# Zero matmuls and a new load order at the start of a hybrid decoder step, and attention scores in two full-height passes

## The chip, the core and the metric

The kernel runs on one core of one Trainium2 chip. The metric is device time in microseconds of one execution, lower is better. Engines are called as the profile calls them: PE is TensorE (matmul), PEld its weight loads, DVE VectorE, ACT ScalarE, POOL GpSimd, SP the engine whose queue issues the DMAs. The trace also gives the clock that TensorE was granted, as a share of 2.4 GHz; its two levels are 1.2 and 2.4 GHz.

## The reference

One layer of a decoder for 1024 prompt tokens and 64 sample tokens (8 requests of 8), model width 1024, float32:

- RMSNorm, then one combined projection into q, k, v of a sliding-window attention (8 heads of 64, 2 key heads) and into the parts of an mLSTM (4 heads);
- sliding-window attention with sinks, where each block of 128 queries reads its own and the previous block of keys:

```python
s = jnp.einsum('bnqhgd,bnkhd->bnhgqk', q, k) * (HEAD_DIM ** -0.5)
s = jnp.where(mask, s, -jnp.inf)
m = jnp.maximum(jnp.max(s, axis=-1, keepdims=True), sink)
p = jnp.exp(s - m)
p = p / (jnp.sum(p, axis=-1, keepdims=True) + jnp.exp(sink - m))
```

- the mLSTM in chunks with a carried state, head norm and output gate; both joined by one output projection and a residual add;
- cross-attention to 256 memory tokens (4 heads of 64), a SwiGLU feed-forward of 2816, a last RMSNorm. The sample tokens do the same with cached keys, values and states.

## The kernel before

Activations lie feature-major (128 features on the partitions, 1088 tokens along the row), cut in columns into `CH` = 384, 384 and 320. Every large product is made of three float32r products: both operands are split exactly into a high and a low part (`split`, L100 to L109: high part by ScalarE, L102 or L108, or by VectorE with a scale, L106; low part by VectorE or GpSimd, L103 or L109), and `mm3` adds high x high, high x low and low x high in PSUM. `mm` (L85) records every matmul, so in the trace products are told apart by their tiles.

Weights come through `load_w` (L111): one DMA into `wraw` (two buffers), then a split into `whi` and `wlo` (two buffers each). `tok_w` does so for the token-major weights `win_a` and `win_b`.

The start (L157 to L203): for each of eight feature tiles the x tile is loaded (L162) and split, even tiles with ScalarE and odd ones with VectorE for the high part. Behind tile 0 the first two weight tiles `win_f[0]` and `win_f[1]` are loaded whole. ScalarE squares the x tiles (L174), GpSimd adds the first half of the squares and VectorE the second (L178). The two first column tiles, in six PSUM accumulators, run along with the arrival of x (144 matmuls). Then a float32 product with ones sums the squares over the features, ScalarE makes rstd of it, and the token-major part begins with `wa = tok_w(win_a, ...)`, whose raw parts use the two `wraw` buffers, and `tok_gemm`.

The mLSTM and the four q tiles follow. In the sliding-window stretch `swa_unit` (L684) does one block of 128 queries and one pair of q tiles, 16 units in the order block, pair. A generator (`wout_mlstm`) gives matmul work that is set between the units, `nfill[u]` pieces behind unit u. The scores of a unit:

```python
for j2 in range(2):
    cs = slice(j2 * 256, j2 * 256 + 256)
    for z, (a, b_) in enumerate(((qh, khi), (qh, klo), (ql, khi))):
        for kv in range(2):
            pr = slice(kv * 64, kv * 64 + 64)
            mm(sc[kv][:, cs], a[pr, j2, :], b_[pr, k0:k0 + 256], z == 0, z == 2)
```

These are twelve matmuls of 64 rows: head 0 of the pair on partitions 0 to 63, head 1 on 64 to 127. VectorE then adds the mask and takes the maxima (L703), ScalarE the exponentials (L622), VectorE scales (L627), TensorE transposes (`pt`, L717), ScalarE copies (`pp`, L718), and the product with the values follows (`o`). `cross_unit` (8 units, each two blocks and one pair of heads) has the same form with `kvhl` in place of the keys: maxima L866, exponentials L887, scales L891, transposes L897. `swa_sample` and `cross_sample` do the sample tokens in float32.

Buffers: slots of one size under a tag; tag `c` has nine, which hold x tiles, keys (`khi`, `klo`), values (`vp`), the mLSTM values, `kvf`, `pp` and later feed-forward operands. `tmp` has ten. PSUM: `mm` three banks, `pt` two, `sc` two, `o` one.

Order: the tile framework orders the instructions of each engine by the order of the program and by when its own model has their operands ready, allocates slots as they come free, and sets all semaphores. Engines then run their queues in that order.

Of the kernel before, what the change touches and what calls it, by code (L numbers as in the profile page):

```python
# [9 lines left out]
F32 = mybir.dt.float32  # L10
# [5 lines left out]
P = 128  # L16
D = 1024
NK = D // P                 # feature tiles of the model width
TP = 1024                   # prompt tokens
TS = 64                     # sample tokens (8 requests x 8)  # L20
T = TP + TS
NB = TP // P                # prompt token blocks
CH = [(0, 384), (384, 768), (768, 1088)]
CHE = [(0, 416), (416, 832), (832, 1088)]   # where the last one ends the kernel
FT = 22                     # feature tiles of the FFN
GROUPS = [(0, 2), (2, 6), (6, 10), (10, 14), (14, 18), (18, 22)]
EPS = 1e-6
NEG = -1.0e30

# columns of the vectors packed by the host  # L30
# [3 lines left out]
# columns of the constants  # L34
C_ID, C_ONE, C_CAUS, C_CAUSS, C_BM, C_M0, C_M1 = 0, 128, 256, 384, 448, 456, 712
C_N = 968
# columns of the constants for the gates
# [5 lines left out]
def tile_hymba_step(  # L43
# [51 lines left out]

    def gcol(base, k):
        return vv[:, base + k:base + k + 1]

# [1 line left out]
    def split(hi, lo, src, scale=None, eng=None):  # L100
        if scale is None:
            A.activation(hi, src, AF.Copy)  # L102
            (eng or V).tensor_tensor(lo, src, hi.bitcast(F32), ALU.subtract)  # L103
        else:
            if eng is V:
                V.tensor_scalar_mul(hi, src, scale)  # L106
            else:
                A.activation(hi, src, AF.Copy, scale=scale)  # L108
            V.scalar_tensor_tensor(lo, src, scale, hi.bitcast(F32), ALU.mult, ALU.subtract)  # L109

# [12 lines left out]
    def load_ahead(srcs):  # L123
        """The weights in the order of their use, each loaded one step ahead of it."""
        todo, ahead = iter(srcs), []

        def step():
            for src, eng in todo:
                ahead.append(load_w(src, 8, eng=eng))
                break  # L130

        def next_w():
            step()
            return ahead.pop(0)

        step()
        return next_w
# [19 lines left out]
    # ================= stage 1: x, split; sums of squares =================  # L157
    nc.scalar.preload_act_table_set("natural_log_exp_and_others")
    xs, xr = [], []
    for k in range(NK):  # L160
        xr.append(slot("cm"[k % 2], [T], name="xraw"))
        nc.sync.dma_start(xr[k], xT[k])  # L162
        hi, lo = slot("x", [T], F32R, name="xhi"), slot("x", [T], F32R, name="xlo")
        split(hi, lo, xr[k], gcol(V_MIX, k), V if k % 2 else A)
        xs.append((hi, lo))
        if k == 0:
            w = load_w(win_f[0], NK)
        if k == 0:
            w1 = load_w(win_f[1], NK)
    nc.sync.dma_start(c, cst)  # L170
    sums = []
    for k in range(NK):
        sq = slot("q", [T], name="sq")
        A.activation(sq, xr[k], AF.Square)  # L174
        if k % 4 == 0:
            sums.append(sq)
        else:
            (G if k < 4 else V).tensor_tensor(sums[-1], sums[-1], sq, ALU.add)  # L178
    rstd = slot("r", [T], name="rstd")
    # the first two tiles run along with the arrival of x  # L180
# [24 lines left out]
    # token-major rstd  # L205
# [19 lines left out]

    def tok_w(src, n, per, tags):
        parts = []
        for k0 in range(0, NK, per):
            tag = tags[k0 // per]
            raw = wp.tile([P, per, n], F32, tag="wraw", name="wrawt", bufs=2)  # L230
            nc.sync.dma_start(raw, src[:, k0:k0 + per, :])
            hi, lo = slot(tag[0], [per, n], F32R, name="wthi"), slot(tag[-1], [per, n], F32R, name="wtlo")
            split(hi, lo, raw)
            parts.append((hi, lo))
        return lambda k: (parts[k // per][0][:, k % per, :], parts[k // per][1][:, k % per, :])
# [11 lines left out]
    wa = tok_w(win_a, 264, 4, "qm")  # L247
# [108 lines left out]
    # rows (block, head) of prompt; rows (head) of sample  # L356
# [40 lines left out]
    # the weight of the state before the block, as rows  # L397
# [33 lines left out]
    # the upper half of the partitions holds the odd heads  # L431
# [20 lines left out]
    # M4: mq pair 0, mq pair 1, mk pair 0, mk pair 1; later the head outputs  # L452
# [4 lines left out]
    # the heads' norm weights with the half of sigmoid(x) = (1 + tanh(x / 2)) / 2  # L457
# [42 lines left out]
    def mlstm_S(blk, m, c0, bc, caus):  # L500
        """S^T[s, t] of the four heads, weighted."""
        dd = bc
        G.tensor_tensor(dd[:m], caus.unsqueeze(1).to_broadcast([m, 4, m]), bc[:m], ALU.subtract)
        for h in range(4):
            A.activation(dd[:m, h, :], dd[:m, h, :], AF.Exp, bias=gg[:m, blk * 4 + h:blk * 4 + h + 1])
        kq = [scps(), scps()]
        for h in range(4):
            pr = slice((h % 2) * 64, (h % 2) * 64 + 64)
            mm(kq[h % 2][:m, (h // 2) * m:(h // 2) * m + m], M4[2 + h // 2][pr, c0:c0 + m], M4[h // 2][pr, c0:c0 + m])
        S = tmp([4, m], name="S")  # L510
        for h2 in range(2):
            V.tensor_tensor(S[:m, h2::2], kq[h2][:m, 0:2 * m].rearrange("p (j t) -> p j t", j=2),
                            dd[:m, h2::2], ALU.mult)
        return S
# [102 lines left out]
    def softmax_pieces(pieces, mx, nbias, es=None):  # L617
        """P = exp(0.125 s + bias) / (sum + es) in place for the (row, piece) scores."""
# [65 lines left out]
    def swa_unit(blk, jp):  # L684
        k0 = max(0, (blk - 1) * P)
        mask = c[:, C_M0:C_M0 + 256] if blk == 0 else c[:, C_M1:C_M1 + 256]
        qhl = tmp([2, 2, P], F32R, name="qhl")
        qh, ql = qhl[:, 0], qhl[:, 1]
        for j2 in range(2):
            split(qh[:, j2, :], ql[:, j2, :], qc[2 * jp + j2][:, blk * P:blk * P + P])  # L690
        sc = [scps(), scps()]
        for j2 in range(2):
            cs = slice(j2 * 256, j2 * 256 + 256)
            for z, (a, b_) in enumerate(((qh, khi), (qh, klo), (ql, khi))):
                for kv in range(2):
                    pr = slice(kv * 64, kv * 64 + 64)
                    mm(sc[kv][:, cs], a[pr, j2, :], b_[pr, k0:k0 + 256], z == 0, z == 2)
# [50 lines left out]
    class Next:  # L748
        """Operands of the GEMM behind a norm: (y * g) split; rstd goes on its output."""
# [68 lines left out]
    for u in range(2 * NB):  # L818
        if u == 0:
            swa_sample()  # L820
        swa_unit(u // 2, u % 2)
# [6 lines left out]
    kvhl = slot("c", [4, 256], F32R, name="kvhl")  # L828
    kvh, kvl = kvhl[:, 0:2], kvhl[:, 2:4]
    split(kvh, kvl, kvf[:, 0:2])  # L830
# [5 lines left out]
    # weights of this stage in the order of their use  # L836
# [31 lines left out]
    def cross_unit(pair, f):  # L868
        """Two blocks of prompt tokens, one pair of heads."""
        bs = slice(pair * 256, pair * 256 + 256)  # L870
        qhl = tmp([2, 256], F32R, name="qhl")
        split(qhl[:, 0], qhl[:, 1], xq[f][:, bs])
        sc = [scps(), scps()]
        for i in range(2):
            ts = slice(i * P, i * P + P)
            for z, (a, b_) in enumerate(((0, kvh), (0, kvl), (1, kvh))):
                for h2 in range(2):
                    pr = slice(h2 * 64, h2 * 64 + 64)
                    mm(sc[h2][:, i * 256:i * 256 + 256], qhl[pr, a, ts], b_[pr, f, :], z == 0, z == 2)
# [168 lines left out]
def _consts():  # L1048
# [19 lines left out]
    # sample window: rows (request of the pair, kv, group, token)  # L1068
# [13 lines left out]
def _tiles(w, cols=None):  # L1082
    """[K, F] -> [F/128, 128, K/128, 128]"""
# [5 lines left out]
def _pack(i):  # L1089
# [23 lines left out]
    for base, g in ((V_MIX, a["g_mix"][0]), (V_CROSS, a["g_cross"][0]), (V_FFN, a["g_ffn"][0]),  # L1113
# [5 lines left out]
    s = a["attn_sinks"][0].reshape(2, 2, 2)          # kv, pair, j2  # L1119
# [56 lines left out]
```

## Time and profile before

| | us |
|---|---|
| median of 3 runs | 1387.66 |
| lowest and highest run | 1380.97 and 1389.8 |
| span of the profiled execution, first to last instruction | 1380.3 |
| TensorE busy in it | 1343.5 (97%) |
| VectorE, ScalarE, GpSimd busy | 622.2, 444.6, 190.3 |
| mean granted clock of TensorE | 0.995 |

The profile is of one execution, and it gives no other time of that execution than its span; the run nearest to it is the lowest of the three. A matmul's duration covers its way through the array, and several are under way at once, so what a matmul costs is read from the distance between starts.

### The profile page before, as it was taken

What the parts mean: (1) busy time and instruction counts of PE and PEld (TensorE: products, weight loads), DVE (VectorE), ACT (ScalarE), POOL (GpSimd) and SP (SyncE); (2) the same over time, 40 slices, a digit from 0 to 9 for tenths busy, and PEclk for the clock granted to TensorE, in tenths of its full rate; (3) what the DMA queues carried; (4) which work ended last, traced back from release to release, by engine and by line L of the source; (5) the groups of instructions that cost most, each with busy time, mean ns of one, the idle gap of its engine ahead of it and who ended that gap; (6) DMA issues with size and microseconds to landing.
All of it is one profiled execution on the core that took longest, in us unless ns stands there. A gap on an engine that the chain in (4) does not pass through costs nothing.

```text
span 1380.3 us, 20544 instructions
## 1 busy us (share of the span) xinstructions
PE 1343.5 (97%) x8352; PEld 1266.2 (92%) x8352; DVE 622.2 (45%) x1373; ACT 444.6 (32%) x1024; POOL 190.3 (14%) x167
## 2 busy tenths in 40 slices
PE   7999999999999898999999999999999999999997
PEld 6999988887888786799999999999999999999997
DVE  7224345467766778835323332332233232423245
ACT  4322332447754666721221011201121121112133
POOL 3000110100003551110111011101110011001123
PEclk9999999999999999999999999999999999999999
DMA  5122413110311224102111111111112120111113
GB/s 228 40 74 62 146 56 121 38 47 16 131 46 57 97 92 163 52 16 62 47 31 62 46 47 31 51 42 46 47 32 61 31 62 31 62 32 50 43 37 124
DMA packets 38807, 88.26 MB, mean 64 GB/s; under 512 B 6593, under 2 KB 14209, under 8 KB 38713
## 3 DMA queue, kind: packets, MB, share of 16 engines
q1 hardware_dynamic: 38713, 86.95, 19.6%
q8 instruction: 66, 1.08, 0.3%
q14 instruction: 28, 0.23, 0.1%
HBM read 79.54 MB, written 7.38 MB: 63 GB/s over the span
## 4 chain that ended last, share of the span: by engine, by line
PE 58%; DVE 3%; ACT 1%; issue 0%; DMA 0%; POOL 0%; DVEq 0%; ACTq 0%; POOLq 0%
PE mm L85 57%; DVE nlo L109 1%; PE o L85 0%; DVE y L955 0%; PE pt L85 0%; DVE nb L866 0%; DVE wlo L103 0%; DMA ck<-cm_k 0%; PE sc L85 0%; ACT sp L887 0%; ACT sq L773 0%; DVE qhl L103 0%; DVE ss L777 0%; DVE yo L1043 0%; PE pt L897 0%
## 5 line engine op out<-in xcount | busy, mean ns | idle before, releaser
L85 PE MATMUL mm<-nhi,wlo 128*128 128x384 f32 (+1 forms) x1056 | 344.4, 326 | 0.0
L85 PE MATMUL mm<-nlo,whi 128*128 128x384 f32 (+1 forms) x1056 | 344.1, 326 | 0.0
L85 PE MATMUL mm<-nhi,whi 128*128 128x384 f32 (+1 forms) x1056 | 344.0, 326 | 0.0
L102 ACT ACTIVATE whi<-wraw 128x1024 fp32r<-128x1024 f32 (+1 forms) x105 | 109.4, 1042 | 345.9 <-PE mm L85 295.1
L85 PEld LDWEIGHTS mm<-nhi,whi 128*128 128x128 f32 x1056 | 198.2, 188 | 0.1
L85 PEld LDWEIGHTS mm<-nhi,wlo 128*128 128x128 f32 x1056 | 198.2, 188 | 0.1
L85 PEld LDWEIGHTS mm<-nlo,whi 128*128 128x128 f32 x1056 | 198.2, 188 | 0.0
L1005 POOL TENSOR_TENSOR gate<-gate,rstd 128x384 f32<-128x384 f32 (+1 forms) x66 | 78.3, 1187 | 656.3 <-ACT gate L1004 656.3
L85 PE MATMUL mm<-hlo,whi 128*128 128x384 f32 (+3 forms) x480 | 157.1, 327 | 0.0
L85 PE MATMUL mm<-hhi,whi 128*128 128x384 f32 (+3 forms) x480 | 156.9, 327 | 0.0
L85 PE MATMUL mm<-hhi,wlo 128*128 128x384 f32 (+3 forms) x480 | 156.9, 327 | 0.0
L103 DVE TENSOR_TENSOR wlo<-wraw,whi 128x1024 fp32r<-128x1024 f32 (+1 forms) x93 | 112.1, 1205 | 45.6 <-ACT whi L102 41.9
L1008 DVE TENSOR_TENSOR h<-mm,gate 128x384 f32<-128x384 f32 (+1 forms) x66 | 35.4, 536 | 193.9 <-PE mm L85 189.0
L1018 DVE TENSOR_TENSOR y<-y,mm 128x384 f32<-128x384 f32 (+1 forms) x120 | 63.6, 531 | 118.6 <-PE mm L85 118.6
L85 PE MATMUL mm<-xhi,whi 128*128 128x384 f32 (+1 forms) x288 | 98.6, 342 | 0.0
L85 PE MATMUL mm<-xlo,whi 128*128 128x384 f32 (+1 forms) x288 | 98.1, 341 | 0.0
L85 PE MATMUL mm<-xhi,wlo 128*128 128x384 f32 (+1 forms) x288 | 97.3, 338 | 0.0
L1002 DVE TENSOR_TENSOR gate<-mm,rstd 128x384 f32<-128x384 f32 (+1 forms) x66 | 35.4, 536 | 123.5 <-PE mm L85 123.5
L85 PEld LDWEIGHTS mm<-hlo,whi 128*128 128x128 f32 x480 | 90.1, 188 | 0.4 <-issue 0.3
L85 PEld LDWEIGHTS mm<-hhi,whi 128*128 128x128 f32 x480 | 90.2, 188 | 0.2 <-issue 0.2
L85 PEld LDWEIGHTS mm<-hhi,wlo 128*128 128x128 f32 x480 | 90.2, 188 | 0.2 <-issue 0.2
L102 ACT ACTIVATE hhi<-h 128x384 fp32r<-128x384 f32 (+1 forms) x66 | 33.2, 503 | 158.7 <-DVE h L1008 158.6
(343 smaller groups left out, 2169.6 us busy)
## 6 DMA issues: line engine op xcount, KB each, us to landing
wraw<-wg SPq DMA_DIRECT2D x22, 512.0 KB
wraw<-wu SPq DMA_DIRECT2D x22, 512.0 KB
wraw<-wd SPq DMA_DIRECT2D x40, 256.0 KB
wraw<-wout SPq DMA_DIRECT2D x32, 256.0 KB
wraw<-win_f SPq DMA_DIRECT2D x13, 512.0 KB
xraw<-xT SPq DMA_DIRECT2D x8, 544.0 KB
y<-xT SPq DMA_DIRECT2D x8, 544.0 KB
o_y<-yo SPq DMA_DIRECT2D x16, 208.0 KB
```

The source lines that it names most:

```text
L85: return TE.matmul(out, lhsT, rhs, start=start, stop=stop)
L102: A.activation(hi, src, AF.Copy)
L103: (eng or V).tensor_tensor(lo, src, hi.bitcast(F32), ALU.subtract)
L109: V.scalar_tensor_tensor(lo, src, scale, hi.bitcast(F32), ALU.mult, ALU.subtract)
L1002: V.tensor_tensor(t, ga, fr[:, c0:c1], ALU.mult)
L1005: G.tensor_tensor(t, t, fr[:, c0:c1], ALU.mult)
L1008: V.tensor_tensor(h, ua, t, ALU.mult)
L1018: V.tensor_tensor(y[d][:, c0:c1], y[d][:, c0:c1], acc, ALU.add)
```

## The change

1. A tile of zeros is multiplied with itself eleven times (128x128, float32) into a PSUM tile before all other matmuls.
2. The first loads are cut and put in order of use: a quarter of weight tile 0, 384 columns of x tile 0, the rest of x tile 0, the rest of weight tile 0, weight tile 1, x tiles 1 to 7. VectorE splits these two weight tiles alone; ScalarE makes the high part of every x tile. The squares are queued behind the last x split on ScalarE, and VectorE does all adds. `tok_w(win_a)` stands ahead of the first products in the program.
3. Scores: the keys are laid twice on the partitions, once per key head (`kst`, by GpSimd), and the query's high part is laid beside its low part in the other half of the partitions (`stack`). One matmul of 128 rows with the key's high parts then gives high x high + low x high, a second one with the low parts high x low + low x low, a term that was left out before. Units run as block pair, pair of q tiles, block. `cross_unit` does the same with `kvs`.

```diff
+IDLE = 11
+    idle = tmp([P], name="idle")
+    V.memset(idle, 0.0)
+    rest = ops([P])
+    for _ in range(IDLE):
+        mm(rest, idle, idle)
...
+    def split_w(raw, parts):
+        hi = wp.tile([P, NK, P], F32R, tag="whi", name="whi", bufs=2)
+        lo = wp.tile([P, NK, P], F32R, tag="wlo", name="wlo", bufs=2)
+        for k0, k1 in parts:
+            V.tensor_copy(hi[:, k0:k1, :], raw[:, k0:k1, :])
+            V.tensor_tensor(lo[:, k0:k1, :], raw[:, k0:k1, :], hi[:, k0:k1, :].bitcast(F32), ALU.subtract)
+        return hi, lo
     for k in range(NK):
         xr.append(slot("cm"[k % 2], [T], name="xraw"))
-        nc.sync.dma_start(xr[k], xT[k])
         hi, lo = slot("x", [T], F32R, name="xhi"), slot("x", [T], F32R, name="xlo")
-        split(hi, lo, xr[k], gcol(V_MIX, k), V if k % 2 else A)
+        if k == 0:
+            raw = first_w(0)
+            nc.sync.dma_start(raw[:, 0:2, :], win_f[0][:, 0:2, :])
+            nc.sync.dma_start(xr[k][:, 0:CH[0][1]], xT[k][:, 0:CH[0][1]])
+            nc.sync.dma_start(xr[k][:, CH[0][1]:T], xT[k][:, CH[0][1]:T])
+            nc.sync.dma_start(raw[:, 2:NK, :], win_f[0][:, 2:NK, :])
+            raw1 = first_w(1)
+            nc.sync.dma_start(raw1, win_f[1])
+            w = split_w(raw, ((0, 2), (2, NK)))
+            for c0, c1 in (CH[0], (CH[0][1], T)):
+                split(hi[:, c0:c1], lo[:, c0:c1], xr[k][:, c0:c1], gcol(V_MIX, k), A)
+            w1 = split_w(raw1, ((0, 2), (2, NK)))
+        else:
+            nc.sync.dma_start(xr[k], xT[k])
+            x_done = split(hi, lo, xr[k], gcol(V_MIX, k), A)
-        if k == 0:
-            w = load_w(win_f[0], NK)
-        if k == 0:
-            w1 = load_w(win_f[1], NK)
...
-        A.activation(sq, xr[k], AF.Square)
+        with tc.issue_after(x_done.ins):
+            A.activation(sq, xr[k], AF.Square)
...
-            (G if k < 4 else V).tensor_tensor(sums[-1], sums[-1], sq, ALU.add)
+            V.tensor_tensor(sums[-1], sums[-1], sq, ALU.add)
+    wa = tok_w(win_a, 264, 4, "qm")
     rstd = slot("r", [T], name="rstd")
...
-    wa = tok_w(win_a, 264, 4, "qm")
...
+    kst = []
+    for kv in range(2):
+        pr = slice(kv * 64, kv * 64 + 64)
+        both = []
+        for src in (khi, klo):
+            t = slot("c", [T], F32R, name="kst")
+            for z in range(2):
+                G.tensor_copy(t[z * 64:z * 64 + 64], src[pr].bitcast(F32))
+            both.append(t)
+        kst.append(both)
+    def stack(src):
+        st = tmp([2, 256], F32R, name="qst")
+        for z in range(2):
+            p_, q_ = slice(z * 64, z * 64 + 64), slice((1 - z) * 64, (1 - z) * 64 + 64)
+            A.activation(st[p_, z], src[p_], AF.Copy)
+            V.tensor_tensor(st[q_, z], src[p_], st[p_, z].bitcast(F32), ALU.subtract)
+        return st
-    def swa_unit(blk, jp):
+    def swa_unit(bp, jp, bi):
+        blk = 2 * bp + bi
+        if bi == 0:
+            for j2 in range(2):
+                qst[j2] = stack(qc[2 * jp + j2][:, bp * 256:bp * 256 + 256])
...
+        for kv in range(2):
+            for j2 in range(2):
+                cs = slice(j2 * 256, j2 * 256 + 256)
+                for z in range(2):
+                    mm(sc[kv][:, cs], qst[j2][:, kv, bi * P:bi * P + P], kst[kv][z][:, k0:k0 + 256],
+                       z == 0, z == 1)
...
-        swa_unit(u // 2, u % 2)
+        swa_unit(u // 4, u // 2 % 2, u % 2)
...
-    kvhl = slot("c", [4, 256], F32R, name="kvhl")
-    kvh, kvl = kvhl[:, 0:2], kvhl[:, 2:4]
-    split(kvh, kvl, kvf[:, 0:2])
+    kvs = [slot("c", [2, 2, 256], F32R, name="kvs") for _ in range(2)]
+    for h2 in range(2):
+        pr, po = slice(h2 * 64, h2 * 64 + 64), slice((1 - h2) * 64, (1 - h2) * 64 + 64)
+        split(kvs[0][pr, h2], kvs[1][pr, h2], kvf[pr, 0:2])
+        for z in range(2):
+            G.tensor_copy(kvs[z][po, h2], kvs[z][pr, h2].bitcast(F32))
...
     def cross_unit(pair, f):
...
-        qhl = tmp([2, 256], F32R, name="qhl")
-        split(qhl[:, 0], qhl[:, 1], xq[f][:, bs])
+        st = stack(xq[f][:, bs])
...
+        for h2 in range(2):
+            for i in range(2):
+                for z in range(2):
+                    mm(sc[h2][:, i * 256:i * 256 + 256], st[:, h2, i * P:i * P + P], kvs[z][:, h2, f, :],
+                       z == 0, z == 1)
```

## Rows read from the trace of the kernel before

**Rows 1.** Busy time by stretch: length, then PE, PEld, DVE, ACT, POOL (instructions), clock, DMA.

```profile
300.00:412.00 112.00, 111.52 (x756) 89.11 (x757) 79.05 (x321) 75.43 (x254) 0.00 (x0) 0.98 0.19 64
...
465.00:575.00 110.00, 99.45 (x661) 80.53 (x661) 88.79 (x193) 71.31 (x179) 35.75 (x26) 0.98 0.34 111
```

**Rows 2.** TensorE's waits: who waited for whom, us in all, times, longest.

```profile
PE sc L85 <- ACT whi L102: 8.0, 1, 8.0
PE pt L897 <- DVE sp L891: 4.2, 5, 1.7
```

**Rows 3.** Timeline, TensorE, first 43 us: start, duration, engine, line, operation.

```profile
12.12 0.53 PE L85 MATMUL mm<-xhi,whi 128*128 128x384 f32 x1
12.44 0.53 PE L85 MATMUL mm<-xlo,whi 128*128 128x384 f32 x1
...
15.39 0.34 PE L85 MATMUL sc<-xhi,whi 128*128 128x384 f32 x1
15.57 0.35 PE L85 MATMUL sc<-xlo,whi 128*128 128x384 f32 x1
...
37.77 3.82 PE L85 MATMUL pt<-sq,c 128*128 128x384 f32 x12
41.65 0.36 PE L85 MATMUL mm<-wthi,xhi 128*128 128x264 f32 x1
42.72 0.39 PE L85 MATMUL mm<-wtlo,xhi 128*128 128x264 f32 x1 [0.71 <-DVE wtlo L103]
```

**Rows 4.** Timeline, first 20 us: ScalarE, VectorE and GpSimd on the x tiles.

```profile
4.77 1.20 ACT L108 ACTIVATE xhi<-xraw,vv 128x1088 fp32r<-128x1088 f32 x1 [2.76 <-DMA xraw<-xT]
...
6.01 1.35 DVE L109 SCALAR_TENSOR_TENSOR xlo<-xraw,vv,xhi 128x1088 fp32r<-128x1088 f32 x1 [2.90 <-ACT xhi L108]
...
9.68 1.11 ACT L174 ACTIVATE sq<-xraw 128x1088 f32<-128x1088 f32 x1 [0.28 <-DMA xraw<-xT]
...
10.87 9.96 POOL L178 TENSOR_TENSOR sq<-sq 128x1088 f32<-128x1088 f32 x3 [9.94 <-ACT sq L174]
...
11.40 7.04 DVE L109 SCALAR_TENSOR_TENSOR xlo<-xraw,vv,xhi 128x1088 fp32r<-128x1088 f32 x2
```

**Rows 5.** Timeline, TensorE: a pair of score matmuls (`khi`, then `klo`) between full ones.

```profile
307.09 0.34 PE L85 MATMUL mm<-xlo,whi 128*128 128x384 f32 x1
307.36 0.38 PE L85 MATMUL sc<-khi,qhl 64*128 64x256 f32 x1
...
307.79 0.44 PE L85 MATMUL mm<-xhi,wlo 128*128 128x384 f32 x1
308.06 0.34 PE L85 MATMUL mm<-xhi,whi 128*128 128x384 f32 x1
```

**Rows 6.** Busy time of `qhl`'s instructions by stretch (PE, PEld, DVE, ACT); full 256-column matmuls.

```profile
300.00:412.00 112.00, 19.73 (x175) 13.71 (x176) 8.10 (x30) 7.67 (x30) 0.98 0.19 64
465.00:575.00 110.00, 9.18 (x96) 6.61 (x96) 5.23 (x8) 2.98 (x8) 0.98 0.34 111
...
147.20 0.28 PE L85 MATMUL mm<-memhi,whi 128*128 128x256 f32 x1
147.32 0.28 PE L85 MATMUL mm<-memlo,whi 128*128 128x256 f32 x1
```

**Rows 7.** Instructions of `qhl`: count, duration ns min/median/max, first and last start.

```profile
L103 DVE TENSOR_TENSOR qhl<-qc,qhl x32: 260/285/293, 292.7 to 405.1; 128x128 fp32r<-128x128 f32 x32
L102 ACT ACTIVATE qhl<-xq x8: 399/417/435, 464.7 to 561.8; 128x256 fp32r<-128x256 f32 x8
L103 DVE TENSOR_TENSOR qhl<-xq,qhl x8: 421/426/1479, 465.1 to 563.4; 128x256 fp32r<-128x256 f32 x8
```

**Rows 8.** Timeline near 418 us: VectorE's scalings beside GpSimd.

```profile
417.75 3.23 DVE L627 TENSOR_SCALAR sp<-sp,l 128x256 f32<-128x256 f32 x4
...
418.33 2.50 POOL L103 TENSOR_TENSOR wlo<-wraw,whi 128x1024 fp32r<-128x1024 f32 x1 [150.65 <-ACT whi L102]
```

**Rows 9.** Busy time of one stretch; behind the five engines stands the granted clock.

```profile
298.20:305.00 6.80, 6.80 (x32) 5.76 (x32) 4.99 (x22) 3.58 (x12) 0.00 (x0) 0.54 0.00 0
```

More of the change, by code (lines that the diff above doesn't have):

```diff
@@ L107, in split @@
             else:
-                A.activation(hi, src, AF.Copy, scale=scale)
+                first = A.activation(hi, src, AF.Copy, scale=scale)
             V.scalar_tensor_tensor(lo, src, scale, hi.bitcast(F32), ALU.mult, ALU.subtract)
+            return first if eng is not V else None
     def load_w(src, nk, nf=P, tag=None, eng=None):
@@ L159, in tile_hymba_step, with first_w @@
     xs, xr = [], []
+    wraw = []
+    def first_w(i):
+        raw = wp.tile([P, NK, P], F32, tag="wraw", name="wraw", bufs=2)
+        wraw.append(raw)
+        return raw
+    def split_w(raw, parts):
[5 more added lines that the diff above has]
+        return hi, lo
     for k in range(NK):
         xr.append(slot("cm"[k % 2], [T], name="xraw"))
-        nc.sync.dma_start(xr[k], xT[k])
         hi, lo = slot("x", [T], F32R, name="xhi"), slot("x", [T], F32R, name="xlo")
-        split(hi, lo, xr[k], gcol(V_MIX, k), V if k % 2 else A)
+        if k == 0:
[13 more added lines that the diff above has]
+            x_done = split(hi, lo, xr[k], gcol(V_MIX, k), A)
         xs.append((hi, lo))
-        if k == 0:
-            w = load_w(win_f[0], NK)
-        if k == 0:
-            w1 = load_w(win_f[1], NK)
     nc.sync.dma_start(c, cst)
@@ L177, in tile_hymba_step, with tok_w @@
         else:
-            (G if k < 4 else V).tensor_tensor(sums[-1], sums[-1], sq, ALU.add)
+            V.tensor_tensor(sums[-1], sums[-1], sq, ALU.add)
+    def tok_w(src, n, per, tags):
+        parts = []
+        for k0 in range(0, NK, per):
+            tag = tags[k0 // per]
+            raw = wp.tile([P, per, n], F32, tag="wraw", name="wrawt", bufs=2)
+            nc.sync.dma_start(raw, src[:, k0:k0 + per, :])
+            hi, lo = slot(tag[0], [per, n], F32R, name="wthi"), slot(tag[-1], [per, n], F32R, name="wtlo")
+            split(hi, lo, raw)
+            parts.append((hi, lo))
+        return lambda k: (parts[k // per][0][:, k % per, :], parts[k // per][1][:, k % per, :])
+    wa = tok_w(win_a, 264, 4, "qm")
     rstd = slot("r", [T], name="rstd")
@@ L224, in tile_hymba_step @@
         G.memset(mvx[i][:, :, :, P:P + 1], 1.0)
[L226 to L235, printed above, removed]
     def tok_gemm(w, b, n, src=None):
@@ L682, in swa_sample @@
                 V.tensor_copy(qc[j][pr, TP:T].rearrange("p (b t) -> p b t", t=8), o[pr, :, kv, j, :])
-    def swa_unit(blk, jp):
+    kst = []
[15 more added lines that the diff above has]
+        return st
+    qst = [None, None]
+    def swa_unit(bp, jp, bi):
[3 more added lines that the diff above has]
+                qst[j2] = stack(qc[2 * jp + j2][:, bp * 256:bp * 256 + 256])
         k0 = max(0, (blk - 1) * P)
         mask = c[:, C_M0:C_M0 + 256] if blk == 0 else c[:, C_M1:C_M1 + 256]
[L687 to L690, printed above, removed]
         sc = [scps(), scps()]
[L692 to L697, printed above, removed]
+        for kv in range(2):
[4 more added lines that the diff above has]
+                       z == 0, z == 1)
         sp = [tmp([2, 256], name="sp") for _ in range(2)]
@@ L870, in cross_unit @@
         bs = slice(pair * 256, pair * 256 + 256)
-        qhl = tmp([2, 256], F32R, name="qhl")
-        split(qhl[:, 0], qhl[:, 1], xq[f][:, bs])
+        st = stack(xq[f][:, bs])
         sc = [scps(), scps()]
[L874 to L879, printed above, removed]
+        for h2 in range(2):
[3 more added lines that the diff above has]
+                       z == 0, z == 1)
         sp = [tmp([2, 256], name="sp") for _ in range(2)]
```

## The prediction

> **What bounds the kernel now.** I read the busy share by stretch first, then TensorE's waits, then the timeline at the start and at the scores. From 300 to 412 us, the sliding-window stretch, TensorE is busy 111.5 of 112 us while VectorE has 79 and ScalarE 75; from 465 to 575, the cross-attention stretch, TensorE is busy 99.5 of 110 and VectorE 88.8 [rows 1]. So the first of the two is TensorE's own and the second is shared between engines. The waits say the same: TensorE's one long wait is the 8.0 us before its first product, and the next, 4.2 us in five pieces, is on VectorE in cross-attention [rows 2]. The feed-forward part behind both is not touched.
>
> **The start, before.** The first product begins at 7.97 us [rows 2]. At 12 us products of 384 columns follow each other every 0.32 us, at 15.4 us every 0.18 us: the clock was at its 1.2 GHz level first and at 2.4 GHz by then [rows 3]. x tile 0 is there at 4.77 us, tile 1 at about 9.68 [rows 4]. GpSimd adds squares from 10.87 to 20.8 us, and beside it two VectorE splits take 7.04 us, where one alone takes 1.35 [rows 4]. The two first column tiles are done at 37.77, the 3.82 us of float32 sums behind them at about 41.6, and the token-major products begin at 41.65, with a pause to 42.72 on a weight split [rows 3].
>
> **Part 1, the zeros.** Eleven float32 products of 128 columns are added. No row shows one. The nearest is the sum over squares: 3.82 us in twelve records for six float32 products of 384 columns, 0.64 us each [rows 3], so 0.21 us for 128 columns at full clock and 0.43 at half. Eleven cost 2.3 to 4.7 us; I take 4.7, since the clock is low then. They need only a memset and lie from about 1 to 5.8 us, inside the 8.0 us in which TensorE waits [rows 2]; they cost nothing unless the first operands come earlier than that. What they can bring is the higher clock for the first real products: between nothing (the zeros don't raise it, or it falls again in the next pause) and half of the 6.9 us that before ran at the lower level, 3.4 us.
>
> **Part 2, the order of the first loads and splits.** The first operands become a quarter of weight tile 0 and 384 columns of x tile 0, split by VectorE (weights) and ScalarE (x). Tile 0 was whole at 4.77 [rows 4]; its first piece comes no later although the small weight piece is ahead of it, and ScalarE needs some 0.5 us, 1.20 us being the whole tile's. So the first product could run at 5.3 to 5.9 instead of 7.97. That alone is worth little: bytes in front of x tile 1 are the same, so it still arrives at 9.7 us and is split by 10.9. From there seven steps remain. A step is 18 products, 6 x (0.175 + 0.175 + 0.147) = 2.98 us at full clock (the 320-column one in proportion), seven are 20.9. With GpSimd's adds gone each step's splits take 1.20 us on ScalarE and 1.35 on VectorE, under half of a step, so TensorE isn't starved again. The end is 10.9 + 20.9 = 31.8, with 0.8 for the wait on the first low part 32.6, against 37.77: 5.2 us. Moving squares behind all the x splits hides them: eight of 1.11 us [rows 4] and six adds of about 1.3 from some 19.7 us on end before 32. The queue of SP is passed by two loads more and by the win_a loads, which wait for the same two buffers as before. The token-major weight is now split ahead of rstd, so the pause from 41.65 to 42.72 shrinks to a normal step of 0.12: 0.9 us [rows 3]. Sum 6.1; for clock not yet up at 10.9 I take off 0.6. **Term: -5.5 us, between -2.5 and -7.5.** All engines behind it to 300 us run against TensorE, so it carries through.
>
> **Part 3, the scores.** Per unit twelve products of 64 rows become eight of 128 rows, 256 columns each; there are 16 sliding-window and 8 cross units. On the chip, a pair of 64-row products set between two full ones costs: the product ahead of it keeps the array 0.27 us instead of 0.18, the pair 0.43, the product behind 0.27 instead of 0.18 [rows 5]; 0.6 us for a sixth of a unit. All score products of the sliding window have TensorE for 19.7 us from 300 to 412 (and some 2 us just before), those of cross-attention for 9.2 [rows 6]. A 128-row product of 256 columns follows every 0.12 us, weights included, where this kernel has them: 147.20, 147.32 [rows 6]. So 16 x 8 x 0.12 = 15.4 against 21.7, and 8 x 8 x 0.12 = 7.7 against 9.2; 6.3 and 1.5 us saved, and some of the 0.09 us at each edge between 64-row and full products besides. I take -6.5 for the sliding window, all of it on the path since nothing else ends there. The range is -2 to -9.
>
> The Trainium skill, TensorEngine Tiling (Array Packing), has two rules that pull apart. Under Theoretical Speedup, two tiles of up to 64 rows may give up to twice the rate, which speaks against folding them into one. Under Key Properties, changing the tiling mode drains the array, which speaks for it. By the first, twelve would cost no more than six; this trace has 19.7 us for 175 records, 0.113 us each [rows 6], which doesn't agree; by the second the edges above are what is seen, and it agrees [rows 5].
>
> **Part 4, what the scores add elsewhere.** stack() works on half the partitions and all 256 columns: two copies and two subtractions, each as long as a 256-column one, 0.417 and 0.426 us [rows 7]. Per two sliding-window units VectorE has 4 x 0.426 = 1.70 instead of 4 x 0.285 = 1.14 [rows 7], ScalarE about as much more: +4.5 us over the stretch on engines with over 30 us of room [rows 1]: nothing on the path. Per cross unit one copy and one subtraction more, 8 x 0.43 = 3.4 us on each of two engines, and VectorE is what TensorE waits for there [rows 1, 2]. If half of VectorE's and a fifth of ScalarE's is on the path, that is +2.4, against 1.5 that TensorE saves and the first bank's maxima that can start after four products rather than twelve: **+0.5, between -3 and +7**. GpSimd gets eight copies for the stacked keys and four for the memory keys. No row has such a copy; the bounds are 1 us each (a tenth of VectorE's work hit) and the 3.3 us of one of its adds [rows 4], 8 to 26 us in all. While GpSimd works, VectorE is slow: four scalings took 3.23 us beside a 2.50 us GpSimd operation [rows 8]. The keys are known by 45 us and slots come free during the mLSTM stretch, where GpSimd has little to do; I take +0.5 (0 to +4) for what VectorE loses there and around 412.
>
> **Sum.** -5.5 - 6.5 + 0.5 + 0.5 = -11 us. The profiled execution has a span of 1380.3 us; the page gives no time around it, and the nearest of the three runs is 1380.97. The median, 1387.66, is 7.4 above the span. The edits don't touch what lies around the span, so I take the same 11 us off the median: about 1376.5 us, 0.8% less.
>
> **Rivals.** *Both attention stretches give in full:* the edges between 64-row and full products count wholly (sliding window -8.5), cross-attention follows TensorE and the earlier maxima (-2.5), the start -6: 1387.7 - 17 = 1371. For it: TensorE is never waited out in the sliding window [rows 1]; against: VectorE's share in cross-attention. *The scores give nothing:* the longer splits and GpSimd's copies take the place of what TensorE saves, and only the start is left: 1382. For it: VectorE at 88.8 of 110 us; against: 33 us of room in the other stretch. *The zeros don't do it:* the clock is low again when x tile 1 comes, and the start is worth 2.5: 1379.5. For it: the granted clock fell to half in 298.2 to 305.0, mean 0.54, right behind a stretch of short products [rows 9]; against: steps from 10.9 us on are dense. *The other side, pairs were side by side:* if two 64-row products had been worth one full one, a unit cost 6 x 0.12 = 0.72 and costs 0.96 now; 24 units lose 5.8 us, and with the longer splits on the path in cross-attention (+3.4) the start's 5.5 is outweighed: 1387.7 - 5.5 + 5.8 + 3.4 = 1391. It decides once the loss in the scores is over 5.5 us; the 0.113 us per product speaks against it. By the Trainium skill's page named above (Theoretical Speedup), it is this one that would hold.
>
> **How the numbers follow.** Forecast 0.40 (own range 1371 to 1381), full gain 0.25, scores nothing 0.17, zeros nothing 0.10, the other side 0.08. A measurement of this kernel tells about 1% from no change: faster means under 1373.8, slower over 1401.5. Of the full gain four fifths lie under 1373.8 (0.20), of the forecast a third (0.13): faster 0.33. Slower needs the other side together with copies of GpSimd at their upper bound: 0.05. The rest, 0.62, is within 1%. The range runs from 1367 to 1388: below it a tenth (both full and a lost fall of the clock, 3.4 us), above it the other side.
>
> **What would show it.** Start: products 0.18 us apart as soon as x tile 1 is split, the two column tiles done near 32 us and token-major products near 36; if products are 0.32 apart there, the zeros failed. Scores: 128x256 products 0.12 us apart, full products around them back at 0.18, the sliding-window stretch some 6 us shorter. Wrong would be: TensorE waiting for the score splits in the sliding window, VectorE slowed by long GpSimd copies beside the softmax, or a cross-attention stretch longer than before by more than 3 us.

## The result, and the profile after

The changed kernel takes 1396.9 us (median of 4 runs, 1395.5 to 1397.0), beside 1385.7 us of the kernel before: ratio 1.0074, 95% interval 1.0052 to 1.0097. It is 11 us slower where 11 us faster was forecast, and lies outside the range of 1367 to 1388. The difference is inside the 1% that the prediction called no change, but its sign is certain. The page of the profiled execution (1397.0 us):

```profile
span 1395.1 us, 20428 instructions
PE 1356.0 (97%) x8278; PEld 1281.8 (92%) x8278; DVE 635.8 (46%) x1389; ACT 458.7 (33%) x1036; POOL 192.2 (14%) x176
...
PEclk9999996989999999999999999999999999999999
```

TensorE is busy 97% of the span, as before. What is new is in the last line: slice 7 (209 to 244 us) ran at 0.6 of full clock, slice 9 at 0.8.

The start, TensorE's timeline:

```profile
1.08 4.84 PE L86 MATMUL o<-idle 128*128 128x128 f32 x22 [1.08 <-DVE idle L98]
5.68 0.42 PE L86 MATMUL sc<-xhi,whi 128*128 128x384 f32 x1
...
33.81 3.82 PE L86 MATMUL pt<-sq,c 128*128 128x384 f32 x12
...
37.23 0.53 PE L86 MATMUL mm<-wthi,xhi 128*128 128x264 f32 x1
```

The zeros take 4.84 us. The tail of their last record reaches to 5.92 us, over the start of the first product at 5.68, which follows them without a wait of its own (before, TensorE waited 8.0 us for its first product [rows 2]). The sums of squares begin at 33.81 instead of 37.77, the token-major products at 37.23 instead of 41.65 [rows 3]. About four microseconds are won here, and they are still there at 215 us: the instruction that begins at 215.03 us below began at 219.03 before.

Then they are lost. Busy time by stretch around the mLSTM of the samples (TensorE, weight loads, VectorE, ScalarE, GpSimd, granted clock), the changed kernel:

```profile
200.00:221.00 21.00, 19.21 (x123) 15.94 (x121) 13.20 (x35) 7.32 (x29) 5.14 (x5) 0.99 0.19 48
221.00:249.00 28.00, 28.00 (x99) 21.94 (x100) 8.66 (x24) 3.14 (x9) 9.10 (x9) 0.52 0.21 72
```

and the kernel before:

```profile
200.00:221.00 21.00, 20.87 (x140) 17.36 (x139) 9.65 (x34) 6.69 (x27) 1.70 (x2) 1.00 0.14 46
221.00:249.00 28.00, 27.33 (x172) 22.20 (x171) 15.83 (x41) 8.93 (x33) 5.52 (x7) 1.00 0.39 124
```

From 221 to 249 us TensorE is busy for all 28 us, and gets 99 records done instead of 172: the granted clock is 0.52, the 1.2 GHz level. Busy time alone wouldn't show it; the count and the clock do. Of 28 us at 0.52 some 28 x 0.48 = 13.4 us are lost, an estimate.

What stands ahead of the fall, VectorE, GpSimd and TensorE in the changed kernel:

```profile
214.84 0.15 DVE L513 COPY rec<-pt 64x2 f32<-64x2 f32 x1 [1.23 <-PE pt L86]
214.93 2.23 POOL L725 CAST kst<-khi 64x1088 fp32r<-64x1088 f32 x2 [11.69 <-PE pt L86]
215.03 1.01 DVE L514 SCALAR_TENSOR_TENSOR rec<-rec 64x4 f32<-64x4 f32 x1
216.07 1.09 DVE L515 TENSOR_TENSOR rec<-rec,g_em 64x4 f32<-64x4 f32 x1
...
219.10 1.16 PE L86 MATMUL sc<-mvs,kz 64*128 64x129 f32 x8 [1.66 <-DVE kz L595]
220.18 0.44 PE L86 MATMUL mm<-xhi,wlo 128*128 128x384 f32 x1
220.56 0.58 PE L86 MATMUL pt<-g_wi,sel 64*128 64x4 f32 x2
```

and VectorE's two instructions in the kernel before:

```profile
219.03 0.15 DVE L481 SCALAR_TENSOR_TENSOR rec<-rec 64x4 f32<-64x4 f32 x1
219.22 0.15 DVE L482 TENSOR_TENSOR rec<-rec,g_em 64x4 f32<-64x4 f32 x1
```

Two of GpSimd's eight copies for the stacked keys, 1.1 us each, got a slot just when VectorE had its small chain to do. Two instructions on 64x4 elements take 1.01 and 1.09 us instead of 0.15, each until a copy ends; `kz` is 1.8 us late, and TensorE waits 1.66 us for it. The Trainium skill, SBUF — State Buffer (SBUF: two separate sides), says that VectorE and GpSimd have one pair of ports that one of them holds for a whole instruction, among others when a VectorE instruction has two inputs in SBUF and GpSimd reads SBUF; the trace agrees: both instructions end with the copies, and took seven times as long.

The sliding window, its output products by line (duration of one, first and last start), before and in the change:

```profile
L85 PE MATMUL o<-pp,vp x128: 379/379/431, 311.0 to 422.8; 128*64 128x256 f32 x128
L86 PE MATMUL o<-pp,vp x128: 378/379/431, 323.4 to 431.8; 128*64 128x256 f32 x128
```

All instructions on the stacked queries, products included, in the 112 us that answer to [rows 6] (TensorE, weight loads, VectorE, ScalarE):

```profile
309.00:421.00 112.00, 22.02 (x120) 17.90 (x120) 11.76 (x28) 11.56 (x28) 0.97 0.19 64
```

One unit's scores on the timeline:

```profile
412.19 1.11 PE L86 MATMUL sc<-kst,qst 128*128 128x256 f32 x8
413.14 0.34 PE L86 MATMUL mm<-chi,whi 128*128 128x384 f32 x1
413.32 0.34 PE L86 MATMUL mm<-clo,whi 128*128 128x384 f32 x1
```

From the first output product to the last it is 108.4 us; before it was 111.8. So 3.4 us are won in the stretch. Inside a run the products stand 0.95 / 8 = 0.119 us apart and the full product behind them keeps the array 0.18 us, both as forecast.

TensorE's waits from 430 to 600 us, where cross-attention is:

```profile
PE pt L954 <- DVE sp L948: 7.2, 6, 2.2
PE mm L86 <- DVE y L1012: 4.7, 4, 3.1
```

The first was 4.2 us in [rows 2]. The last products of all, before and in the change:

```profile
L85 PE MATMUL mm<-hhi,wlos x48: 279/348/356, 1329.3 to 1370.9; 128*128 128x416 f32 x32, 128*128 128x256 f32 x16
L86 PE MATMUL mm<-hhi,wlos x48: 279/349/356, 1344.0 to 1385.6; 128*128 128x416 f32 x32, 128*128 128x256 f32 x16
```

From the last output product of the sliding window to the last product of all it was 948.1 us before (422.8 to 1370.9) and is 953.8 now (431.8 to 1385.6).

### The profile page after: what moved, and what is told of

Its sections match the earlier page's. It is cut to its first block, busy times and chain, and to the rows that moved or that the text cites. A ratio compares the mean times of both kernels' runs of the same rounds, so it can differ in the third digit from the quotient of the medians.

```text
span 1395.1 us, 20428 instructions
## 1 busy us (share of the span) xinstructions
PE 1356.0 (97%) x8278; PEld 1281.8 (92%) x8278; DVE 635.8 (46%) x1389; ACT 458.7 (33%) x1036; POOL 192.2 (14%) x176
## 4 chain that ended last, share of the span: by engine, by line
PE 87%; DVE 6%; ACT 3%; issue 1%; DMA 1%; POOL 0%; SPq 0%; DVEq 0%; ACTq 0%; POOLq 0%
PE mm L86 76%; PE sc L86 3%; PE o L86 3%; PE pt L86 3%; PE pt L773 1%; DVE nb L925 1%; DVE nb L941 1%; DVE nhl L116 1%; DMA xraw<-xT 1%; DVE wlo L110 1%; DVE qst L735 0%; PE pt L954 0%; DVE sp L660 0%; ACT whi L109 0%; DVE nlo L116 0%
```

## The experiments

All times are medians, beside runs of the kernel before on the same chip. The experiments ran on three chips, where before took 1384.5 us (the first two here and both with late copies), 1385.4 (copies alone, copies on ScalarE, half splits, cross-attention alone) and 1385.2 (the last two), so a difference between runs of two chips can be off by about 0.9 us for that alone. The theory from the two traces was that the copies hold VectorE, TensorE pauses, its clock falls in the sparse stretch that follows, and cross-attention pays for its longer splits; the rivals were the earlier start, and the order and slots that the new tiles bring.

**The start alone.** The scores, keys and splits of before are put back; zeros, first loads and split order stay.

```diff
-    kst = []
...
-                    mm(sc[kv][:, cs], qst[j2][:, kv, bi * P:bi * P + P], kst[kv][z][:, k0:k0 + 256], ...)
+            for z, (a, b_) in enumerate(((qh, khi), (qh, klo), (ql, khi))):
...
```

> This is the start of the change alone (zeros, first loads, order of the splits) with the scores of before. Theory A (GpSimd's eight copies for the stacked keys, which lie in the mLSTM of the samples, hold VectorE, TensorE pauses for about 2 us, and its clock falls to the 1.2 GHz level for 27 us): no copies here, so no fall between 215 and 255 us; 1380 to 1383 us, 4 to 7 less than before, mean granted clock 0.994 or more. Theory B (the fall comes from the earlier start, which shifts the sparse stretch of the mLSTM): the fall is here too, 1394 to 1398 us, mean clock about 0.984.

1377.5 us, ratio 0.9947 (0.9927 to 0.9968), 6.9 us under the 1384.5 of before and below the 1380 to 1383 expected; mean clock of the profiled run 0.995, of the other three 0.995, 0.992 and 0.990. As theory A has it, the trace has no fall of the clock at 221 to 249 us.

```profile
221.00:249.00 28.00, 27.91 (x176) 22.10 (x174) 12.70 (x39) 6.77 (x23) 5.52 (x7) 1.00 0.27 88
```

**The scores alone.** The loads, splits and squares of the start are those of before, without zeros.

```diff
-    for _ in range(IDLE):
-        mm(rest, idle, idle)
...
-        with tc.issue_after(x_done.ins):
-            A.activation(sq, xr[k], AF.Square)
+        A.activation(sq, xr[k], AF.Square)
```

> This is the score part alone (stacked keys and queries) with the start of before. Theory A (GpSimd's copies in the mLSTM make the fall of the clock): the fall is here, some 13 us lost there, 1 to 2 won in the sliding window, 5 to 6 lost in cross-attention: 1400 to 1405 us, mean clock 0.984 or less. Theory B (the fall comes from the earlier start): no fall, 1390 to 1393 us, mean clock 0.994.

1401.9 us, ratio 1.0123 (1.0107 to 1.0139), mean clock 0.984: theory A again. In its trace TensorE waits the same 1.66 us for `kz`, and the clock falls behind it. The earlier start isn't needed for the fall.

**Copies alone.** The start alone, with the eight copies back in their place, read by nothing.

```diff
+    kst = []
+    for kv in range(2):
...
+                G.tensor_copy(t[z * 64:z * 64 + 64], src[pr].bitcast(F32))
```

> The start of the change with the scores of before, and GpSimd's eight key copies besides, which no score reads. The run of the start alone was 1377.5 us. If the copies make the fall of the clock in the mLSTM of the samples, by holding VectorE and by the order that TensorE's products get beside them: the fall of 24 to 27 us is here, 1391 to 1394 us, mean clock 0.984 to 0.986. If the fall needs the new score products or the new splits: no fall, 1377 to 1380 us, mean clock 0.995.

1390.8 us, ratio 1.0051 (1.0035 to 1.0067): 13.3 us more than the start alone (12.3 if each is taken beside before on its own chip), by copies that take some 8.9 us (four times 2.23) of an engine with little else to do. All ten runs had a mean clock of 0.983 to 0.986. The same chain:

```profile
214.47 2.23 POOL L725 CAST kst<-khi 64x1088 fp32r<-64x1088 f32 x2 [11.69 <-PE pt L86]
214.57 1.01 DVE L514 SCALAR_TENSOR_TENSOR rec<-rec 64x4 f32<-64x4 f32 x1
```

and the stretch:

```profile
221.00:249.00 28.00, 27.77 (x97) 21.64 (x97) 11.24 (x26) 3.27 (x9) 8.34 (x7) 0.52 0.36 121
```

**Copies on ScalarE.** The whole change, another engine for the eight copies.

```diff
-                G.tensor_copy(t[z * 64:z * 64 + 64], src[pr].bitcast(F32))
+                A.activation(t[z * 64:z * 64 + 64], src[pr], AF.Copy)
```

> The whole change, with the eight key copies on ScalarE instead of GpSimd. If the fall comes from GpSimd beside VectorE: `rec` 0.15 us, no wait of TensorE on kz, no fall before 300 us, some 14 us less than the change, 1381 to 1384 us, mean clock 0.993. If the slots that the copies take, or the order alone, make it: the fall stays, 1393 to 1398 us.

1385.3 us, ratio 0.9997 (0.9977 to 1.0017): 11.6 us less than the change, a little above the 1381 to 1384 expected. The chain:

```profile
213.91 2.24 ACT L725 ACTIVATE kst<-khi 64x1088 fp32r<-64x1088 f32 x2 [6.74 <-PE pt L86]
214.09 0.15 DVE L514 SCALAR_TENSOR_TENSOR rec<-rec 64x4 f32<-64x4 f32 x1
214.28 0.15 DVE L515 TENSOR_TENSOR rec<-rec,g_em 64x4 f32<-64x4 f32 x1
```

and the stretch:

```profile
221.00:249.00 28.00, 28.00 (x142) 22.85 (x141) 10.91 (x32) 14.22 (x33) 4.37 (x6) 0.82 0.38 122
```

The copies start at the same point of the chain and last as long (2.24 us for two); VectorE's instructions beside them take 0.15 us again. So it is GpSimd beside VectorE, not the copying, that holds VectorE. TensorE's order differs too: behind the first `kz` products stand one full product, `sel`, ten full ones, `hh` and three, so this run takes away the pause and the order of the change together. The clock still fell for a part of the stretch in this execution (0.82). ScalarE's other six copies, from 230 to 237 us, don't make that by themselves: in the run of the three good parts below the same copies lie at 231 to 238 us, and its trace has the clock at 1.00 from 221 to 249. What does isn't shown.

**Late copies.** The whole change, the copies on GpSimd behind its last operation of the mLSTM.

```diff
-                G.tensor_copy(t[z * 64:z * 64 + 64], src[pr].bitcast(F32))
+                with tc.issue_after(last_g.ins):
+                    G.tensor_copy(t[z * 64:z * 64 + 64], src[pr].bitcast(F32))
```

> The whole change, but GpSimd's eight copies for the stacked keys are issued behind its last operation of the mLSTM. Theory A (the copies there hold VectorE and so make the fall of the clock): `rec` takes 0.15 us again instead of 1.01, no fall between 215 and 255 us, 11 to 14 us less than the change: 1383 to 1386 us, mean clock 0.993 or more. Theory B (the earlier start makes the fall): 1395 to 1398 us, mean clock 0.984. Theory C (the scheduler's other order or the slots of the new tiles make the pause, not the copies): 1394 to 1398 us with `rec` short and the pause still there.

1389.2 us, ratio 1.0024 (0.9991 to 1.0057), and none of the theories as stated: ten runs from 1381.7 us at a mean clock of 0.994 to 1398.8 at 0.980. The profiled one is the longest, its chain

```profile
215.64 0.15 DVE L514 SCALAR_TENSOR_TENSOR rec<-rec 64x4 f32<-64x4 f32 x1
```

and its stretch:

```profile
221.00:249.00 28.00, 28.00 (x108) 21.52 (x108) 8.55 (x25) 3.14 (x9) 5.01 (x6) 0.57 0.26 85
```

No copy, no held instruction, no wait of TensorE in the stretch, and yet the clock is at 0.57. So the pause isn't needed for the fall. What this kernel still shares with the change is the order in which the scheduler set TensorE's products: behind the first `kz` products stand one full product, `sel`, three full ones, `hh` and seven, where the start alone has six, `hh`, `sel` and ten. But this order doesn't make the fall by itself, as the next run shows, and it isn't needed either: the traces of the half splits (0.50 from 226 to 241 us) and of no zeros (0.54 from 229 to 243 us) have the order of before, no copies, and a fall of some 15 us. The stretch, with its short products on `kz`, is on the edge. Where the pause and the order came together (the change, the scores alone, the copies alone) the fall was in all three traces, and all 18 runs had a mean clock of 0.986 or less. How much each of the two weighs isn't shown: the order comes with the copies.

**Late copies, old cross-attention.** As the last, with cross-attention of before.

```diff
-        st = stack(xq[f][:, bs])
+        qhl = tmp([2, 256], F32R, name="qhl")
+        split(qhl[:, 0], qhl[:, 1], xq[f][:, bs])
...
```

> As the run with the late copies, and cross-attention's scores, splits and keys are those of before. If the 5 to 6 us that the change lost from the end of the sliding window to the end of cross-attention come from the longer splits (one copy and one subtraction more per unit, on the chain that TensorE waits for there): 5 to 6 us less than the run with the late copies, 1377 to 1380 us. Rival (the loss there is a shift of slots and order that comes with the stage ahead): within 2 us of the run with the late copies.

1380.0 us, ratio 0.9969 (0.9950 to 0.9988), 9.2 us less than the last. The mean clocks of both spread widely (0.985 to 0.993 here, 0.980 to 0.994 there); their three lowest runs, all with a mean clock of 0.992 or more, differ by 5.0 us on average (1377.4 and 1382.4), as expected. Its trace has the order of the last, and no fall:

```profile
221.00:249.00 28.00, 27.70 (x172) 22.12 (x171) 14.21 (x39) 7.76 (x28) 4.23 (x6) 1.00 0.27 85
```

**Half splits.** The start alone, and each split of a cross unit in two halves of 64 rows, as long and as many as in the change; products as before.

```diff
-        split(qhl[:, 0], qhl[:, 1], xq[f][:, bs])
+        for z in range(2):
+            p_ = slice(z * 64, z * 64 + 64)
+            split(qhl[p_, 0], qhl[p_, 1], xq[f][p_, bs])
```

> The start of the change with the scores of before, and each split of a cross-attention unit done in two halves of 64 rows, so that ScalarE and VectorE do as many and as long instructions as in the change, while TensorE's score products are those of before. If the longer splits are what the cross-attention stretch lost (from the last output product of the sliding window to the last product of all it was 946.5 to 948.2 us with the old cross-attention and 953.7 to 955.4 with the new): 5 to 6 us more than the start alone, 1382 to 1384 us. If it is the slots of the new key tiles or the order of the new score products: 1377 to 1379 us.

1382.6 us, ratio 0.9993 (0.9971 to 1.0016): 5.0 us more than the start alone (4.1 beside before on each chip), at or a little under the 5 to 6 expected. TensorE's first waits from 430 to 600 us, the start alone:

```profile
PE pt L931 <- DVE sp L925: 3.0, 5, 1.1
PE mm L86 <- DVE y L989: 2.6, 3, 1.8
```

and with half splits:

```profile
PE pt L933 <- DVE sp L927: 4.5, 5, 2.0
PE mm L86 <- DVE y L991: 3.9, 4, 2.1
```

Both grow though not one product was changed: the splits are in front of VectorE's softmax and additions. From the last output product to the last product of all this trace takes 952.0 us, the start alone 946.6.

**Cross-attention alone.** The change without its sliding-window part.

```diff
-    kst = []
...
-            qst[j2] = stack(qc[2 * jp + j2][:, bp * 256:bp * 256 + 256])
+            split(qh[:, j2, :], ql[:, j2, :], qc[2 * jp + j2][:, blk * P:blk * P + P])
...
```

> The start of the change with the sliding-window scores of before and the cross-attention of the change; no key copies in the mLSTM. If cross-attention's loss is its own: no fall of the clock before 290 us, and 6 to 7 us more than the start alone, 1383 to 1385 us. If the loss is carried over from the new sliding-window part (slots of the stacked keys, order): 1377 to 1379 us.

1387.5 us, ratio 1.0022 (1.0002 to 1.0041): 10 us more than the start alone (9.0 beside before on each chip), above the 6 to 7 expected. The waits are near those of the change (4.7 on `y` again):

```profile
PE pt L941 <- DVE sp L935: 6.4, 7, 1.9
```

The loss is there without the new sliding window: it is cross-attention's own. From the last output product to the last product of all this trace takes 955.6 us; the five traces with the new cross-attention have 953.6 to 955.6, the six with the old one 946.6 to 949.3. Its runs had mean clocks of 0.989 to 0.993, the half splits' mostly 0.992 to 0.996, so a part of the 4.9 us between these two is the clock; what the rest is stays open.

**The three good parts.** Start and sliding window of the change, copies on ScalarE, cross-attention of before; the edits stand above.

> The start and the sliding-window scores of the change, the key copies on ScalarE, and the cross-attention of before. If the three terms add up: the run with the copies on ScalarE (1385.3 us) less the 5 to 7 us of the new cross-attention, 1378 to 1380 us; where the clock doesn't fall in the mLSTM of the samples, 1374 to 1376. If the sliding window's gain of 2 to 3 us is real beside the start alone (1377.5 us), runs with a mean clock of 0.995 lie at 1373 to 1375; if the new scores give nothing, none lies under 1376.

1377.8 us, ratio 0.9949 (0.9930 to 0.9969): faster than both kernels, and no different from the start alone. None of its eight runs was under 1376.2 us.

```profile
L86 PE MATMUL o<-pp,vp x128: 379/379/634, 308.4 to 417.1; 128*64 128x256 f32 x128
```

The stretch takes 108.7 us; in the start alone it took 111.8 (306.0 to 417.8). Of the 3.1 us won, 2.4 are given back ahead of it: its first output product is that much later, 0.6 of it already at the sums of squares (33.55 against 32.91 us). Behind it 2.7 more are lost, though cross-attention is that of before: 949.3 us to the last product of all, the longest with the old one, against 946.6. So by its own expectation the new sliding window gave this kernel nothing.

**No zeros.** The start alone with `IDLE = 0`; the zeros are no part of the reference's work.

```diff
-IDLE = 11
+IDLE = 0
```

> The start of the change with the scores of before, without the eleven products on zeros (none of the work of the reference is left out). If the zeros only bring the higher clock earlier: first product still at about 5.7 us, products 0.32 us apart until the clock rises, two column tiles done 2.5 to 3.5 us later than with zeros (33.8 us in the change), 1380 to 1381 us. If the clock rises as early without them, since the steps from the third x tile on are dense anyway: within 1 us of the start alone, 1377 to 1378 us.

1381.1 us, ratio 0.9974 (0.9958 to 0.9990), as the first theory had it in time but not in place. TensorE's timeline, and one stretch of its windows:

```profile
5.32 0.69 PE L86 MATMUL sc<-xhi,whi 128*128 128x384 f32 x1 [5.32 <-ACT xhi L115]
...
6.46 0.52 PE L86 MATMUL sc<-xhi,wlo 128*128 128x384 f32 x1
6.78 0.52 PE L86 MATMUL sc<-xhi,whi 128*128 128x384 f32 x1
...
34.11 3.82 PE L86 MATMUL pt<-sq,c 128*128 128x384 f32 x12
```

```profile
229.00:243.00 14.00, 14.00 (x54) 11.29 (x53) 3.77 (x8) 1.06 (x1) 4.95 (x6) 0.54 0.53 167
```

The first product starts at 5.32 us, 0.36 before that of the change, whose first high part ScalarE had ready at 5.43: there the zeros were in its way. The first products are 0.32 us apart, the lower level. The sums of squares start at 34.11 us. But with the same zeros they start at 32.91 us in the trace of the start alone and at 34.38 in that of the late copies, where products were 0.32 us apart again at 11 us:

```profile
32.91 3.82 PE L86 MATMUL pt<-sq,c 128*128 128x384 f32 x12
...
34.38 3.82 PE L86 MATMUL pt<-sq,c 128*128 128x384 f32 x12
```

So the 1.2 us between this run and the start alone lie inside what one start differs by between executions. Beside before the two kernels are at -4.1 and -6.9 us, with intervals that overlap, and this trace has the fall in the mLSTM of the samples besides (229 to 243 us), with the order of before and no copies. What the zeros are worth is not shown.

## Why the prediction was wrong

**The copies on GpSimd: the step that failed.** "slots come free during the mLSTM stretch, where GpSimd has little to do; I take +0.5 (0 to +4) for what VectorE loses there and around 412." Their total, 8.9 us, was inside the 8 to 26 estimated, and VectorE loses 1.8 us at the place that counts. But the copies alone cost 13.3 us (12.3 beside before on each chip), where 0 to 4 was forecast. The term counted VectorE's loss as the price. It should have asked who waits for VectorE there and what TensorE's clock does when its work thins out. Both halves were on the table: four scalings at 3.23 us beside a GpSimd operation [rows 8], and a clock at 0.54 behind short products [rows 9]. The second was used for the start only.

**Cross-attention: +0.5 forecast, +5.7 measured** (948.1 to 953.8 us), inside the range of -3 to +7. The mechanism was named and its share was sized too small: "half of VectorE's and a fifth of ScalarE's" 3.4 us is 2.4, where half splits alone cost 4.1 to 5.0 of the 6.8 us that the two engines get. They work one after the other ahead of each unit's scores, so most of it can be on the path. The prediction's own sign of being wrong, a stretch longer by more than 3 us, was there. The 1.5 us of TensorE and the earlier maxima don't show.

**The sliding window: -6.5 forecast, -3.4 measured** in its stretch, and nothing that shows in the time of the kernel (the three good parts). The sum set 21.7 us, busy time of the old products, against 15.4, the spacing of the new ones. These are two measures: a record's busy time has a tail that lies under the next product. In one measure, busy time in answering stretches of 112 us, the new products take 22.02 us in 120 records where the old took 19.73 in 175 [rows 6]. Nor was the price of an old product known from it. Inside a run of them, in the trace of before, two stand side by side:

```profile
341.51 0.28 PE L85 MATMUL sc<-khi,qhl 64*128 64x256 f32 x1
341.52 0.28 PE L85 MATMUL sc<-klo,qhl 64*128 64x256 f32 x1
341.63 0.28 PE L85 MATMUL sc<-khi,qhl 64*128 64x256 f32 x2
```

One pair starts 0.12 us behind the other, so six pairs of a unit take 0.72 us in a run, where the eight new products take 0.96. By these rows the products alone saved nothing in a run; that the 3.4 us come from the edges between 64-row and full products is argued, not shown. The 0.12 us of a new product and the 0.18 us behind it were right; the difference of the two sums was not the saving.

**The start: -5.5 forecast, -6.9 measured** (by the interval some -10 to -4). The zeros (4.84 us for 4.7) and the first product (5.68 for 5.3 to 5.9) came as forecast. The column tiles ended at 33.81 instead of about 32 and the token-major products began at 37.23 instead of 36, since x tile 1 was there at 11.07 us and split by 12.28, where the sum had 9.7 and 10.9:

```profile
11.07 1.21 ACT L115 ACTIVATE xhi<-xraw,vv 128x1088 fp32r<-128x1088 f32 x1 [4.42 <-DMA xraw<-xT]
```

In the start alone that tile was there at 10.14 us, and the tiles ended at 32.91. That the zeros cost nothing didn't hold exactly: the first operands came earlier than they ended. The size of the term was right; that the zeros had a share in it is not shown.

Along the two traces the terms add up. The change is 4.0 us ahead at 215 us, 12.4 behind at the first output product (323.4 against 311.0), 9.0 behind at the last one, and 14.7 at the last product; the spans differ by 14.8 (1395.1 and 1380.3). Of the 16.4 us lost between the first two points the fall is 13.4 by the estimate above, the wait for `kz` 1.7, and some 1.6 are in a second fall, from 306.8 to 317.0 us in the changed kernel (10.20 us at 0.54), where before it was 6.8 us [rows 9]: 3.4 us more at about half.

```profile
306.80:317.00 10.20, 10.20 (x41) 9.49 (x42) 3.48 (x20) 1.24 (x2) 0.00 (x0) 0.54 0.01 2
```

The medians differ by 11.2 us only, since the profiled execution of before is near the lowest of its runs.

**The rivals.** The other side had the right sign. Its premise holds inside a run, as the rows at 341 us show; the prediction set 0.113 us per record against it and against the first of the two rules that it cites, but that was busy time again. Its price did not come: the sliding window got 3.4 us shorter, not 16 x 0.24 = 3.8 longer, and the kernel was slower for another reason, the copies. "All engines behind it to 300 us run against TensorE, so it carries through" held only as long as the clock did. No case had a fall of the clock in the mLSTM, and so the range ended too low.

## What to carry to other kernels

Copies that an idle engine does aren't free: look at which small chain of VectorE they land beside, and which product waits for that chain. Where TensorE has a stretch of short products between waits, read its granted clock and its count of records, not its busy time, before you add anything near it. Take a saving from one measure, start to start on both sides, never busy time against spacing. And take no worth of a microsecond from one pair of executions: here the same start ended 1.5 us apart.

## What the runs showed of the hardware

A VectorE instruction of 0.15 us with two inputs in SBUF took 1.01 to 1.09 us beside a GpSimd copy, to the end of the copy; beside a ScalarE copy of the same size it took 0.15. Two products of 64 rows started together (341.51 and 341.52 us), and in a run such pairs stood 0.12 us apart, like single products of 128 rows. TensorE's clock went to its 1.2 GHz level for some 24 to 27 us while TensorE had work all the time: 28.00 of 28 us busy at 0.52 or 0.57, with a pause of 1.66 us ahead of it or with none. That stretch is on the edge: the kernel with late copies ran at a mean clock of 0.980 or 0.994 from one execution to the next, 17 us apart (1381.7 and 1398.8), which is more than any edit here was worth. The kernel before spreads too, from 1380.5 us at 0.997 to 1391.6 at 0.989 in 31 runs on one chip.
